# The bias table of a decoder trunk: 128 replicas copied from DRAM by GpSimd's queue instead of from one SBUF partition by ScalarE's

## The chip, the cores and the metric

The kernel runs on one core of one Trainium2 chip. The metric is device time in microseconds (us). Before the change three runs took 2225.4, 2230.37 and 2230.59 us, with a median of 2230.37 us. The engines of a core are named as in the profile: PE (TensorE, matrix products), PEld (its weight loads), DVE (VectorE), ACT (ScalarE), POOL (GpSimd) and SP (SyncE, which here only starts transfers). "ACTq" and "SPq" in a row are the queues of ACT and SP themselves: rows in which the engine's instruction stream is held by a transfer that it issues.

## The reference, cut to what matters

The reference is a trunk of two layers, 512 tokens of width 1024. Each layer has three sub-layers, each followed by a layer norm: a gated feed-forward block (FFN), a mixer of parallel head groups (sparse attention, spatial gating, a state-space scan), and a second FFN. Each sub-layer's input and output are scaled and shifted by vectors that come from a conditioning vector `c` through a large matrix `ada_w`.

```
mod = (silu(c) @ ada_w[l] + ada_b[l]).reshape(Bn, N_SUB, 3, D_MODEL)
h = x * (1.0 + scale[:, 0]) + shift[:, 0]
y = swiglu(h, ffn_w1[l, 0], ffn_w3[l, 0], ffn_w2[l, 0])
x = layer_norm(ALPHA * x + 0.5 * (1.0 + gate[:, 0]) * y, ...)
...
bias = rel_bias[rel_bucket(query position - key position)]   # 32 buckets, 8 heads
```

The bias of attention depends only on the distance between query and key and on the head. It is the same for both layers.

## The kernel before, in words

All matrix products are made of three products of split operands (`mm3`, lines 120 to 123): a high part and a low remainder of each side. The high part of a weight tile is made by ACT (`whi`, line 103), the low part by DVE (`wlo`, line 105), from a tile `raw` of 128 x 1024 that SP's queue has loaded. `raw` has four buffers.

An FFN (function `ffn`, 22 inner tiles in two halves of 11) does per inner tile f: two loads and splits (`w1`, `w3`), two projections of 24 matmuls each, then the gate: a tanh on ACT (line 292), two operations on DVE (lines 293 and 294, tile `th`), a high part on ACT (line 297, `ghi`) and a low part on DVE (line 298, `glo`). The weights of the next f are fetched and split while PE works on this one. After the 11 tiles of a half the products with `w2` follow (tile `y`), whose weights are first multiplied by a gain on DVE (line 101).

Beside that a background generator (`make_bg`) is advanced once per f. In the first FFN it has 71 parts over 19 calls: 63 belong to seven conditioning vectors (per vector eight loads of 512 KB of `ada_w`, each followed by a dot product on DVE at line 155, and a closing part), and eight belong to `make_bias`. `make_bias` stands behind the fifth vector, so that it runs in the second half of the first FFN. It multiplies the 33 x 8 bias table by a one-hot matrix of distances (line 390), copies the 8 x 640 result to the SBUF tile `row` (line 391), one head per partition, and then writes for each head 128 copies of its row of 640 numbers to the DRAM tensor `lane` (line 395), one transfer per part. The mixers later load from `lane` a 128 x 512 tile `T` per head in which each partition's row is shifted by one (line 88, called from `lane_load`); the replicas make that possible with one transfer. Everything that `make_bias` makes is needed in the mixer only.

A scheduler orders the instructions of each engine in advance; within an engine they then start in that order. The reciprocal roots of the layer norm run on POOL (line 219), which has nothing else to do before the first mixer.

Of the kernel before, what the change touches and what calls it, by code (L numbers as in the profile page):

```python
# [10 lines left out]
F32 = mybir.dt.float32  # L11
# [19 lines left out]
BLANE = 640  # L31
# [20 lines left out]
def kernel(ctx: ExitStack, tc: tile.TileContext, a: dict, out: bass.AP,  # L52
                             subs=((0, 0), (0, 1), (0, 2), (1, 0), (1, 1), (1, 2))):
    nc = tc.nc
    V, S, G, PE = nc.vector, nc.scalar, nc.gpsimd, nc.tensor
# [10 lines left out]
    dram = ctx.enter_context(tc.tile_pool(name="dram", bufs=1, space=DRAM))  # L66
# [10 lines left out]
    def big(s):  # L77
        return bp.tile([128, 1024], F32, tag="b", name=nm(s))

    def tiny(s, n, dt=F32):  # L80
        rot = s in ("mx", "sm", "fc", "st", "mv", "rs", "nr", "gst", "ss")
        return (t4 if rot else t1).tile([128, n], dt, tag=f"t_{s}", name=nm(s))

    def bank(k, s):
        return psp[k].tile([128, 512], F32, tag=k, name=nm(s))

    def load(dst, src):
        nc.sync.dma_start(dst, src)

    def bcast_row(src, n):  # L90
        return bass.AP(tensor=src.tensor, offset=src.offset, ap=[[0, 128], [1, n]])
# [6 lines left out]
    def wsplit(src, n=1024, gain=None):  # L98
        raw = raw_t(src, n)
        if gain is not None:  # L100
            V.tensor_mul(raw, raw, gain)  # L101
        hi = wp.tile([128, 1024], F32R, tag="hi", name=nm("whi"))
        S.copy(hi[:, :n], raw[:, :n])  # L103
        lo = wp.tile([128, 1024], F32R, tag="lo", name=nm("wlo"))
        V.tensor_sub(lo[:, :n], raw[:, :n], hi[:, :n].bitcast(F32))  # L105
        return hi, lo
# [15 lines left out]
        PE.matmul(o, lh, rl, start=False, stop=False)  # L122
        PE.matmul(o, ll, rh, start=False, stop=last)  # L123

    # constants
    cst = const.tile([128, 512], F32, name="cst")
    load(cst, a["cst"])
    ident = cst[:, 0:128]
# [18 lines left out]
        V.scalar_tensor_tensor(csil, c_th, 1.0, csil, op0=ALU.add, op1=ALU.mult)  # L147
        cond["c"] = csil

    # adaLN vectors, as columns  # L150
    mods = {}

    def ada_dot(acc, raw, l, v, k):
# [37 lines left out]
        V.tensor_mul(BB, sc, BB)  # L191
        V.tensor_add(BB, BB, sh)

    # modulated, transposed and split operand of the next projection
    def spread(b, z, P, banks):
        tiles = []
        for q in range(2):
            ps = bank(banks[q], "hps")
            for i in range(4):
                k = 4 * q + i  # L200
                PE.transpose(ps[:, i * 128:(i + 1) * 128], z[:, k * 128:(k + 1) * 128], ident)
            tiles.append(ps)
        for q in range(2):
            t = slab("hsum", "q")
            t3 = t.rearrange("p (k t) -> p k t", k=4)
            for i in range(4):
                sl = slice(i * 128, (i + 1) * 128)
                k = slice(4 * q + i, 4 * q + i + 1)
                if k.start in DVE_MOD:
                    V.tensor_scalar(t[:, sl], tiles[q][:, sl], P["GA"][:, k], P["BB"][:, k], op0=ALU.mult, op1=ALU.add)  # L210
                else:
                    S.activation(t[:, sl], tiles[q][:, sl], AF.Identity, bias=P["BB"][:, k], scale=P["GA"][:, k])
            hh = hT_hi[:, b, 4 * q:4 * q + 4, :]
            S.copy(hh, t3)
            V.tensor_sub(hT_lo[:, b, 4 * q:4 * q + 4, :], t3, hh.bitcast(F32))  # L215
# [161 lines left out]
        flush(P)  # L377
        renew(P)

    # T5 bias by distance, causal  # L380
    def make_bias():
        rb = tiny("rb", 8)
        load(rb[0:32, :], a["rel_bias"])
        V.memset(rb[32:33, :], NEG)
        oh = big("oh")
        load(oh[0:33, 0:BLANE], a["onehot"])
        row = big("row")
        for q, n in ((0, 512), (1, 128)):
            ps = bank("Y", "rowps")
            PE.matmul(ps[0:8, :n], rb[0:33, :], oh[0:33, q * 512:q * 512 + n], start=True, stop=True)  # L390
            V.tensor_copy(row[0:8, q * 512:q * 512 + n], ps[0:8, :n])
        d = dram.tile([8, 128, BLANE], F32, name="lane")
        for h in range(8):
            yield
            S.dma_start(d[h], row[h:h + 1, 0:BLANE].unsqueeze(1).to_broadcast([1, 128, BLANE]))
        lane.append(d)

    def gelu2(dst, src, n):
# [7 lines left out]
    def mixer(l, P, last, lane, params):  # L406
# [15 lines left out]
        G.affine_select(w3v, w3v, pattern=[[0, 4], [1, 128]], compare_op=ALU.is_ge, fill=0.0, base=0,  # L422
                        channel_multiplier=-1)

        # token-major columns
        wa = [wsplit(a["wA"][l, :, c * 852:c * 852 + n], n) for c, n in ((0, 852), (1, 852), (2, 568))]
        wb = [wsplit(a["wB"][l, :, c * 1024:(c + 1) * 1024]) for c in range(2)]
        dtx, gts = tiny("dtx", 16), tiny("gts", 96)
# [36 lines left out]
            project(ps, wsplit(a["wS"][l, i]))  # L465
            return ps

        # work for the tensor engine in small parts, put between those of the attention
        pre = {}

        def fetch(i):
# [11 lines left out]
                    yield  # L483
            return ps

        # state-space inputs
        def conv(i, y):
            ps = proj(i)
            V.tensor_scalar(y, ps, cw[:, i * 4 + 3:i * 4 + 4], cw[:, 24 + i:25 + i], op0=ALU.mult, op1=ALU.add)
            for j in range(1, 4):  # L490
                V.scalar_tensor_tensor(y[:, j:], ps[:, :T - j], cw[:, i * 4 + 3 - j:i * 4 + 4 - j], y[:, j:],
                                       op0=ALU.mult, op1=ALU.add)
            th = slab("cth", "q")
            S.activation(th, y, AF.Tanh)
            V.scalar_tensor_tensor(y, th, 1.0, y, op0=ALU.add, op1=ALU.mult)
# [21 lines left out]
        def pair(t):  # L517
            return [t[:, 0:512], t[:, 512:1024]]
# [15 lines left out]
            S.activation(y, ps, AF.Tanh, scale=0.5)  # L534
            V.scalar_tensor_tensor(y, y, 1.0, ps, op0=ALU.add, op1=ALU.mult)

        # spatial gating
        def spatial(i):
            if not og:
                og.extend(pair(big("og")))  # L540
            ps = yield from proj_parts(8 + i)
            u = og[i]
            S.copy(u, ps)
            gelu2(u, u, 512)
            sv = bank("Y", "sv")
            for b in range(4):
                for j in range(2):
                    g = 2 * i + j
                    PE.matmul(sv[j * 64:(j + 1) * 64, b * 128:(b + 1) * 128],
                              gv[b // 2][:, (b % 2) * 256 + g * 64:(b % 2) * 256 + (g + 1) * 64],  # L550
                              wsT[:, g * 128:(g + 1) * 128], start=True, stop=True)
            t = slab("svb", "q")
            V.tensor_add(tok(t, 0, 4), tok(sv, 0, 4),
                         bs[:, i * 128:(i + 1) * 128].unsqueeze(1).to_broadcast([128, 4, 128]))
            V.scalar_tensor_tensor(u, t, 0.5, u, op0=ALU.mult, op1=ALU.mult)

        # queries, stacked high over low (low over high for the second group); keys: high parts in both halves, low once
        Q, K = {}, {}
        lo_half, hi_half = slice(0, 64), slice(64, 128)

# [34 lines left out]
        between = [({"h": hidden, "q": query, "k": key}[c[0]], int(c[1])) for c in CORE_FILL.split()]  # L595
# [3 lines left out]
                f, i = between.pop(0)  # L599
                f(i)  # L600

        # step sizes and their sums
        dt, aa = tiny("dt", 16), tiny("aa", 16)
        u, r, z2, pl = tiny("du", 16), tiny("dr", 16), tiny("dz", 16), tiny("dp", 16)
        V.scalar_tensor_tensor(u, dtx, -1.0, dtx, op0=ALU.mult, op1=ALU.max)
# [6 lines left out]
        for d in (15, 13, 11, 9, 7, 5, 3):  # L612
# [15 lines left out]
                  start=False, stop=True)  # L628
        cs = tiny("cs", 16)
        V.tensor_copy(cs, cps[:, 0:16])  # L630

        # token-major inputs and states
        Xt = pair(big("Xt"))
        for i in range(2):
            ps = bank("H", "xtp")
# [13 lines left out]
        for c in range(2):  # L649
            for g in range(2):  # L650
                cb = bank("H", "cb")
                for j in range(2):
                    h = 2 * g + j
# [4 lines left out]
                    for n, part_ in enumerate(a2):  # L658
                        PE.matmul(o[:, 128:256], part_[:, k0 + 4:k0 + 5].to_broadcast([128, 128]), trio_r[:, 0:128],
                                  start=False, stop=(n == 1))  # L660
# [5 lines left out]
                          start=True, stop=True)  # L666
# [10 lines left out]
                for j in range(2):  # L677
                    h = 2 * g + j
# [75 lines left out]
        for q in range(2):  # L754
            PE.matmul(ps[:, 0:64], w2k[:, q * 128:(q + 1) * 128], gT[:, q * 128:q * 128 + 64],
                      start=(q == 0), stop=(q == 1))
# [235 lines left out]
        flush(P)  # L992
        renew(P)

    # start
    P0 = {"GA": tiny("GA", 8), "BB": tiny("BB", 8)}
    ab = [tiny(f"ab{j}", 8) for j in range(2)]
    acc = [tiny(f"acc{j}", 8) for j in range(2)]
# [79 lines left out]
    for n, (l, s) in enumerate(subs):  # L1078
        last = n == len(subs) - 1
        P = {}  # L1080

        def params():
            norm_par(l, s, P)
            if (l, s, 2) in mods:
                gate_par(l, s, P)
            if not last and (*subs[n + 1], 0) in mods:
                next_par(l, s, *subs[n + 1], P)

        if s == 1:
            if not lane:  # L1090
                for _ in make_bias():
                    pass
            need(l, s, 2)
            if not last:
                need(*subs[n + 1], 1)
                need(*subs[n + 1], 0)
            cond.clear()
            mixer(l, P, last, lane, params)
        else:
            if share.get(n) and "c" not in cond:  # L1100
                silu_c()
            after_mixer = n > 0 and subs[n - 1][1] == 1
            ffn(l, s, P, last, make_bg(n, P), (2, 0) if after_mixer and QORDER[0] == 3 else (0, 2), params,
                feed if n == 0 else None)
# [87 lines left out]
```

## Time and profile before

| | before |
|---|---|
| runs, us | 2225.4, 2230.37, 2230.59 |
| median, us | 2230.37 |
| span of the profiled execution, us | 2225.3 |
| PE busy | 2099.0 us, 94% |
| DVE busy | 1345.0 us, 60% |
| ACT busy | 776.2 us, 35% |
| POOL busy | 24.1 us, 1% |
| mean granted TensorE clock | 0.978 |

The page gives the span as the profiled execution's time; it is 0.1 us under the fastest run and 5.1 us under the median. PE is busy nearly all the time, so what can be gained lies where PE is not busy. The page's second part shows the busy tenths in 40 slices of 55.6 us. PE has 9 almost everywhere, apart from the first slice (6), the third (7), the last (7) and the sixth to eighth (4, 5, 7), which are the stretch from 278 to 445 us. The granted clock of these three reads 7, 7, 8 where it is 9 elsewhere. This stretch is where `make_bias` runs.

### The profile page before, as it was taken

What the parts mean: (1) busy time and instruction counts of PE and PEld (TensorE: products, weight loads), DVE (VectorE), ACT (ScalarE), POOL (GpSimd) and SP (SyncE); (2) the same over time, 40 slices, a digit from 0 to 9 for tenths busy, and PEclk for the clock granted to TensorE, in tenths of its full rate; (3) what the DMA queues carried; (4) which work ended last, traced back from release to release, by engine and by line L of the source; (5) the groups of instructions that cost most, each with busy time, mean ns of one, the idle gap of its engine ahead of it and who ended that gap; (6) DMA issues with size and microseconds to landing.
All of it is one profiled execution on the core that took longest, in us unless ns stands there. A gap on an engine that the chain in (4) does not pass through costs nothing.

```text
span 2225.3 us, 26047 instructions
## 1 busy us (share of the span) xinstructions
PE 2099.0 (94%) x10024; PEld 1667.4 (75%) x10024; DVE 1345.0 (60%) x2416; ACT 776.2 (35%) x1351; POOL 24.1 (1%) x34
## 2 busy tenths in 40 slices
PE   6979945799999999999999999999999999999997
PEld 5868834588766688888888878888876668888886
DVE  6784612768676686544766645566867676453363
ACT  4221201343455652222334222224345565222232
POOL 0000000000000000000000000000000000000000
PEclk9999977899999999999999999999999999999999
DMA  8763778622421146345445635532241113223331
GB/s 326 222 224 104 228 77 77 198 95 86 152 67 48 39 160 206 108 143 151 136 139 186 184 104 170 168 114 90 90 147 67 48 39 114 95 95 96 102 96 38
DMA packets 93480, 279.71 MB, mean 126 GB/s; under 512 B 19211, under 2 KB 23563, under 8 KB 93356
## 3 DMA queue, kind: packets, MB, share of 16 engines
q1 hardware_dynamic: 92204, 275.43, 38.1%
q10 hardware_dynamic: 1152, 2.62, 3.5%
q8 instruction: 79, 1.29, 0.2%
q14 instruction: 45, 0.37, 0.1%
HBM read 273.27 MB, written 4.74 MB: 125 GB/s over the span
## 4 chain that ended last, share of the span: by engine, by line
PE 74%; DMA 12%; DVE 8%; issue 3%; ACT 2%; ACTq 1%; POOL 0%; SPq 0%; DVEq 0%; POOLq 0%
PE h L122 9%; PE h L121 9%; PE h L123 9%; PE y L121 8%; PE y L123 8%; PE y L122 7%; DMA raw<-in_ada_w_dram 7%; DMA raw<-in_w_dram 3%; PE pj L121 3%; PE pj L122 3%; PE pj L123 3%; PE op L900 3%; PE tp L890 2%; PE S L860 2%; DVE raw L155 2%
## 5 line engine op out<-in xcount | busy, mean ns | idle before, releaser
L121 PE MATMUL h<-hT_hi,whi 128*128 128x512 f32 (+1 forms) x1488 | 561.6, 379 | 60.5 <-ACT whi L103 55.8
L103 ACT CAST whi<-raw 128x1024 fp32r<-128x1024 f32 (+1 forms) x306 | 317.9, 1046 | 719.8 <-issue 197.7
L123 PE MATMUL h<-hT_hi,wlo 128*128 128x512 f32 (+1 forms) x1488 | 561.6, 377 | 0.4 <-DVE wlo L105 0.4
L122 PE MATMUL h<-hT_lo,whi 128*128 128x512 f32 (+1 forms) x1488 | 561.7, 377 | 0.3 <-DVE hT_lo L215 0.3
L105 DVE TENSOR_TENSOR wlo<-raw,whi 128x1024 fp32r<-128x1024 f32 (+1 forms) x306 | 370.5, 1215 | 222.8 <-ACT whi L103 222.0
L121 PEld LDWEIGHTS h<-hT_hi,whi 128*128 128x128 f32 x1488 | 281.4, 189 | 113.5 <-ACT whi L103 57.3
L123 PEld LDWEIGHTS h<-hT_hi,wlo 128*128 128x128 f32 x1488 | 281.7, 189 | 53.7 <-DVE wlo L105 2.5
L122 PEld LDWEIGHTS h<-hT_lo,whi 128*128 128x128 f32 x1488 | 281.9, 189 | 51.4 <-DVE hT_lo L215 0.7
L155 DVE CUSTOM_DVE_ANT_0 raw<-raw,csil 128x1024 f32<-128x1024 f32 x144 | 174.8, 1221 | 199.9 <-DMA raw<-in_ada_w_dram 199.1
L121 PE MATMUL y<-whi,ghi 128*128 128x512 f32 x576 | 228.2, 396 | 30.5 <-DVE th L294 26.1
L122 PE MATMUL y<-wlo,ghi 128*128 128x512 f32 x576 | 227.1, 394 | 1.8 <-DVE wlo L105 1.8
L123 PE MATMUL y<-whi,glo 128*128 128x512 f32 x576 | 226.6, 393 | 0.0
L101 DVE TENSOR_TENSOR raw<-raw,G 128x1024 f32<-128x1024 f32 x86 | 104.6, 1222 | 85.2 <-DMA raw<-in_w_dram 85.0
L121 PEld LDWEIGHTS y<-whi,ghi 128*128 128x128 f32 x576 | 109.9, 191 | 57.8 <-DVE th L294 30.3
L297 ACT CAST ghi<-th 128x512 fp32r<-128x512 f32 x88 | 54.5, 620 | 240.7 <-DVE th L294 230.4
L122 PEld LDWEIGHTS y<-wlo,ghi 128*128 128x128 f32 x576 | 109.8, 191 | 25.3 <-DVE wlo L105 2.8
L123 PEld LDWEIGHTS y<-whi,glo 128*128 128x128 f32 x576 | 109.7, 190 | 23.1
L121 PE MATMUL pj<-hT_hi,whi 128*128 128x512 f32 x288 | 118.5, 411 | 0.0
L123 PE MATMUL pj<-hT_hi,wlo 128*128 128x512 f32 x288 | 113.5, 394 | 0.0
L122 PE MATMUL pj<-hT_lo,whi 128*128 128x512 f32 x288 | 113.1, 393 | 0.0
L294 DVE TENSOR_TENSOR th<-th,h 128x512 f32<-128x512 f32 x88 | 60.0, 683 | 41.4 <-PE h L123 40.3
L892 ACT COPY pt<-tp 128x512 f32<-128x512 f32 (+2 forms) x96 | 54.6, 581 | 85.3 <-PE tp L890 76.5
(288 smaller groups left out, 2564.0 us busy)
## 6 DMA issues: line engine op xcount, KB each, us to landing
raw<-in_w_dram SPq DMA_DIRECT2D x264, 512.0 KB, 3.7
raw<-in_ada_w_dram SPq DMA_DIRECT2D x144, 512.0 KB, 4.5
raw<-in_wS_dram SPq DMA_DIRECT2D x36, 512.0 KB, 4.2
raw<-in_cw_dram SPq DMA_DIRECT2D x16, 512.0 KB, 4.1
raw<-in_wo_dram SPq DMA_DIRECT2D x16, 512.0 KB, 3.5
T<-lane SPq DMA_DIRECT2D x16, 256.0 KB, 4.0
lg<-in_ln_g_dram SPq DMA_DIRECT2D x6, 512.0 KB, 6.9
lb<-in_ln_b_dram SPq DMA_DIRECT2D x6, 512.0 KB, 6.8
```

The lines of the kernel that those rows point to most:

```text
L101: V.tensor_mul(raw, raw, gain)
L103: S.copy(hi[:, :n], raw[:, :n])
L105: V.tensor_sub(lo[:, :n], raw[:, :n], hi[:, :n].bitcast(F32))
L121: PE.matmul(o, lh, rh, start=first, stop=False)
L122: PE.matmul(o, lh, rl, start=False, stop=False)
L123: PE.matmul(o, ll, rh, start=False, stop=last)
L155: V.tensor_tensor_reduce(out=raw, in0=raw, in1=cond["c"], scale=0.5, scalar=0.0, op0=ALU.mult, op1=ALU.add, accum_out=acc[:, k:k + 1])
L294: V.tensor_mul(th, th, h3)
L297: S.copy(hi, th)
L860: PE.matmul(o, Q[g, i][r, qs], K[br][1][r, :nk], start=False, stop=True)
L892: S.copy(pt[0:n, :], tp[0:n, :])
L900: PE.matmul(op[r, :], v, pt[0:n, g * 256:(g + 1) * 256], start=(br == 0), stop=(br == 2 and kb == qb))
```

## The change

The 8 x 640 result in SBUF is copied once to a DRAM tensor `table` (20 KB, one transfer), and the eight transfers that write the 128 replicas per head read their row from there, by an access pattern that names the same 640 numbers 128 times. All nine are issued by GpSimd's queue; ACT issues none. (The rest of the diff removes comments and leaves blank lines.)

```diff
             PE.matmul(ps[0:8, :n], rb[0:33, :], oh[0:33, q * 512:q * 512 + n], start=True, stop=True)
             V.tensor_copy(row[0:8, q * 512:q * 512 + n], ps[0:8, :n])
+        t = dram.tile([8, BLANE], F32, name="table")
+        G.dma_start(t[:, :], row[0:8, 0:BLANE])
         d = dram.tile([8, 128, BLANE], F32, name="lane")
         for h in range(8):
             yield
-            S.dma_start(d[h], row[h:h + 1, 0:BLANE].unsqueeze(1).to_broadcast([1, 128, BLANE]))
+            G.dma_start(d[h], bcast_row(t[h], BLANE))
         lane.append(d)
```

The lines behind it move by two: line 395 becomes 397, and the transfer of the table is line 393.

On ACT, in the second half of the first FFN, before the change (`whi` is the high part of a weight tile, `th` and `ghi` belong to the gate):

```order
L103 CAST whi_2059<-raw_2057 128x1024
L297 CAST ghi_1913<-th_1909 128x512
L395 DMA lane<-row_1923 128x1x640 x2
L292 ACTIVATE th_1995<-h_337_1933 128x512
L395 DMA lane<-row_1923 128x1x640
L297 CAST ghi_1999<-th_1995 128x512
L395 DMA lane<-row_1923 128x1x640 x3
L103 CAST whi_2065<-raw_2063 128x1024
L292 ACTIVATE th_2069<-h_348_2007 128x512
L395 DMA lane<-row_1923 128x1x640
L297 CAST ghi_2073<-th_2069 128x512
L395 DMA lane<-row_1923 128x1x640
```

Six of the eight transfers stand ahead of the cast of the second weight tile of the next f (`whi_2065`). The same place on ACT after the change:

```order
L103 CAST whi_2061<-raw_2059 128x1024
L297 CAST ghi_1913<-th_1909 128x512
L103 CAST whi_2067<-raw_2065 128x1024
L292 ACTIVATE th_1997<-h_337_1935 128x512
L103 CAST whi_2145<-raw_2143 128x1024
L297 CAST ghi_2001<-th_1997 128x512
L103 CAST whi_2151<-raw_2149 128x1024
L292 ACTIVATE th_2071<-h_348_2009 128x512
```

The eight transfers are gone from ACT, and the casts of the next weight tiles stand between the steps of the gate (the tile that was `whi_2065` is `whi_2067` here).

On DVE, from the copy of the bias row on, before the change (`ISA` at line 155 is the dot product of a loaded tile of `ada_w`):

```order
L391 COPY row_1923<-rowps_1927 8x128
L155 ISA raw_2088,mod_360_2079<-raw_2088,csil_112 128x1024
L155 ISA mod_360_2079 128x1
L155 ISA raw_2161,mod_360_2079<-raw_2161,csil_112 128x1024
L155 ISA mod_360_2079 128x1
L155 ISA raw_2164,mod_360_2079<-raw_2164,csil_112 128x1024
L155 ISA mod_360_2079 128x1
L155 ISA raw_2167,mod_360_2079<-raw_2167,csil_112 128x1024
L155 ISA mod_360_2079 128x1
L293 SCALAR_TENSOR_TENSOR th_1995<-th_1995,h_337_1933 128x512
L294 TENSOR_TENSOR th_1995<-th_1995,h_338_1934 128x512
```

The gate's two operations stand behind four dot products in a row. The same place on DVE after the change:

```order
L391 COPY row_1923<-rowps_1927 8x128
L155 ISA raw_2090,mod_360_2081<-raw_2090,csil_112 128x1024
L155 ISA mod_360_2081 128x1
L105 TENSOR_TENSOR wlo_2069<-raw_2065,whi_2067 128x1024
L293 SCALAR_TENSOR_TENSOR th_1997<-th_1997,h_337_1935 128x512
L155 ISA raw_2163,mod_360_2081<-raw_2163,csil_112 128x1024
L155 ISA mod_360_2081 128x1
L155 ISA raw_2166,mod_360_2081<-raw_2166,csil_112 128x1024
L155 ISA mod_360_2081 128x1
L294 TENSOR_TENSOR th_1997<-th_1997,h_338_1936 128x512
```

Now the first of the two stands behind one dot product and the second behind three, and the low part of the next weight tile has moved ahead of them.

On POOL, before its first reciprocal root (`mv`, line 219, which becomes the same line after), after the change:

```order
L393 DMA table<-row_1923 8x640
L397 DMA lane<-table 128x640 x8
L219 ISA
L219 TENSOR_TENSOR mv_2701<-mv_2701,mhalf 128x1
```

Before the change POOL had no transfer here; now its first reciprocal root stands behind nine of them. The eight copies of the heads follow each other with no other instruction between them.

## Rows read from the trace of the kernel before

**Rows 1.** Busy time of each engine in five stretches, from the windows view: start and end, length, PE, PEld, DVE, ACT and POOL busy us (with the count of instructions), granted TensorE clock as a share, mean DMA share, GB/s.

```profile
140.00:180.00 40.00, 26.94 (x110) 21.27 (x109) 26.06 (x27) 10.04 (x11) 0.00 (x0) 0.87 0.39 129
180.00:280.00 100.00, 100.00 (x440) 81.84 (x439) 55.05 (x76) 24.10 (x28) 0.00 (x0) 1.00 0.57 177
300.00:400.00 100.00, 43.74 (x161) 33.38 (x160) 28.10 (x41) 11.57 (x15) 0.00 (x0) 0.71 0.84 98
310.00:340.00 30.00, 1.00 (x2) 0.50 (x2) 5.46 (x8) 2.16 (x3) 0.00 (x0) 0.50 0.69 72
400.00:440.00 40.00, 27.26 (x102) 21.05 (x101) 30.63 (x35) 11.73 (x15) 0.00 (x0) 0.79 0.58 177
```

**Rows 2.** PE in order of time, from the timeline: the last matmul before the two long gaps and the first one behind each (start, duration, and in brackets the idle time before it with what ended it).

```profile
301.99 0.39 PE L123 MATMUL h<-hT_hi,wlo 128*128 128x512 f32 x1
339.00 0.80 PE L121 MATMUL h<-hT_hi,whi 128*128 128x512 f32 x1 [36.63 <-ACT whi L103]
...
346.79 0.39 PE L123 MATMUL h<-hT_hi,wlo 128*128 128x512 f32 x1
362.26 0.79 PE L121 MATMUL h<-hT_hi,whi 128*128 128x512 f32 x1 [15.08 <-ACT whi L103]
```

**Rows 3.** ACT and its queue in order of time from 273 us on.

```profile
273.64 1.05 ACT L103 CAST whi<-raw 128x1024 fp32r<-128x1024 f32 x1 [3.89 <-issue]
278.27 0.62 ACT L297 CAST ghi<-th 128x512 fp32r<-128x512 f32 x1 [3.58 <-DVE th L294]
280.79 9.52 ACTq L395 DMA_DIRECT2D lane<-row  x2
290.41 0.60 ACT L292 ACTIVATE th<-h 128x512 f32<-128x512 f32 x1 [11.53 <-issue]
290.44 1.05 ACTq L395 DMA_DIRECT2D lane<-row  x1
327.85 0.62 ACT L297 CAST ghi<-th 128x512 fp32r<-128x512 f32 x1 [36.84 <-DVE th L294]
327.86 10.01 ACTq L395 DMA_DIRECT2D lane<-row  x3
337.91 1.04 ACT L103 CAST whi<-raw 128x1024 fp32r<-128x1024 f32 x1 [9.44 <-issue]
338.02 11.58 ACTq L395 DMA_DIRECT2D lane<-row  x1
338.86 0.59 ACT L292 ACTIVATE th<-h 128x512 f32<-128x512 f32 x1
349.64 0.62 ACT L297 CAST ghi<-th 128x512 fp32r<-128x512 f32 x1 [10.19 <-issue]
349.66 11.46 ACTq L395 DMA_DIRECT2D lane<-row  x1
361.16 1.99 ACT L103 CAST whi<-raw 128x1024 fp32r<-128x1024 f32 x2 [10.91 <-issue]
```

**Rows 4.** DVE in order of time from 280 to 390 us, the rows whose wait was ended by a transfer.

```profile
307.76 1.22 DVE L155 CUSTOM_DVE_ANT_0 raw<-raw,csil 128x1024 f32<-128x1024 f32 x1 [25.87 <-DMA raw<-in_ada_w_dram]
320.07 1.23 DVE L155 CUSTOM_DVE_ANT_0 raw<-raw,csil 128x1024 f32<-128x1024 f32 x1 [11.07 <-DMA raw<-in_ada_w_dram]
325.19 1.23 DVE L155 CUSTOM_DVE_ANT_0 raw<-raw,csil 128x1024 f32<-128x1024 f32 x1 [3.89 <-DMA raw<-in_ada_w_dram]
386.06 1.23 DVE L155 CUSTOM_DVE_ANT_0 raw<-raw,csil 128x1024 f32<-128x1024 f32 x1 [15.97 <-DMA raw<-in_ada_w_dram]
```

**Rows 5.** The transfers from 281 to 387 us: q10 is ACT's queue, q1 is SP's (packets, MB, share of the time of 16 DMA engines in this stretch), then issues with their count, KB each and median us to landing.

```profile
q10 hardware_dynamic: 1152, 2.62, 73.4%
q1 hardware_dynamic: 1248, 4.55, 11.6%
...
raw<-in_ada_w_dram SPq DMA_DIRECT2D x6, 512.0 KB, 22.5
lane<-row ACTq DMA_DIRECT2D x8, 320.0 KB, 26.4
```

**Rows 6.** The transfers from 220 to 260 us, in the same form.

```profile
q1 hardware_dynamic: 3674, 9.09, 79.2%
...
raw<-in_ada_w_dram SPq DMA_DIRECT2D x10, 512.0 KB, 4.6
```

**Rows 7.** The transfers from 36 to 50 us, among them two (`lg`, `lb`) in which 128 partitions read the same row of 4 KB from DRAM.

```profile
DMA packets 1999, 5.11 MB, mean 365 GB/s; under 512 B 307, under 2 KB 819, under 8 KB 1998
...
q1 hardware_dynamic: 1998, 5.10, 94.5%
...
raw<-in_w_dram SPq DMA_DIRECT2D x2, 512.0 KB, 10.5
lg<-in_ln_g_dram SPq DMA_DIRECT2D x1, 512.0 KB, 10.5
lb<-in_ln_b_dram SPq DMA_DIRECT2D x1, 512.0 KB, 10.4
```

**Rows 8.** The transfers from 2195 to 2225 us, which write the result from 128 partitions to DRAM.

```profile
q1 hardware_dynamic: 1152, 2.10, 18.7%
...
out_dram<-x_sb SPq DMA_DIRECT2D x8, 256.0 KB, 2.0
```

**Rows 9.** The chain of waits that ended last, from 270 to 400 us, its shares by line.

```profile
by line: DMA raw<-in_ada_w_dram 58.0%; ACTq L395 15.6%; issue 9.5%; DVE raw L155 5.7%; DMA raw<-in_w_dram 3.3%; DVE wlo L105 2.8%; ACT whi L103 2.4%; DVE th L294 2.1%; DVE th L293 0.9%; ACT ghi L297 0.9%; DVE row L391 0.6%; DVE glo L298 0.5
```

**Rows 10.** POOL's first reciprocal root, from the timeline of POOL.

```profile
467.29 0.55 POOL L219 TENSOR_TENSOR mv<-mv,mhalf 128x1 f32<-128x1 f32 x1 [466.78 <-DVE mv L218]
```

**Rows 11.** The first loads that read the replicas, from the timeline of SP's queue.

```profile
481.64 1.81 SPq L88 DMA_DIRECT2D T<-lane  x4
```

## The prediction

> **What bounds the kernel now.** I read the busy tenths of the page first: PE is busy nearly everywhere but in one stretch in the first quarter, and the granted clock falls there too. So the second view is the windows around that stretch [rows 1]. From 180 to 280 us PE is 100% busy at clock 1.00 and does 440 matmuls; from 300 to 400 us it does 161 at a mean of 0.71, and from 310 to 340 us two, at 0.50, which is the 1.2 GHz level of the 1.2 and 2.4 GHz. The reader is to see that this is lost PE time in the middle of an FFN that otherwise keeps PE full, not a stage with another limit. The two transitions from projections to the `w2` products (140 to 180 and 400 to 440 us) lose less, and about the same: 110 and 102 matmuls in 40 us.
>
> Third, the timeline of PE: it runs dry at 302 us, and both long gaps (36.63 and 15.08 us) are ended by the same thing, the cast of a weight tile on ACT [rows 2]. Fourth, the timeline of ACT says why the cast is late [rows 3]. ACT's own work is small, but the eight transfers of line 395 hold its stream for 9.52 + 1.05 + 10.01 + 11.58 + 11.46 = 43.6 us, 5.5 us each, and the `ghi` cast at 327.85 waits 36.84 us for DVE. So fifth, DVE: its dot products wait 25.87, 11.07, 3.89 and 15.97 us for loads of `ada_w` [rows 4], and the gate stands behind them in order. Sixth, the transfers: from 281 to 387 us the 16 engines spend 73.4% of their time on ACT's queue for only 2.62 MB, while the loads of `ada_w` take 22.5 us to land [rows 5], against 4.6 us in an undisturbed stretch [rows 6]. Two things therefore hold PE up, one behind the other: ACT's stream is held by issuing, and the loads that DVE needs crawl because the DMA engines are full of replicas. The chain of waits of this stretch has them both: 58.0% loads of `ada_w`, 15.6% ACT's queue and 9.5% "issue" [rows 9].
>
> How slow the replicas are: 2.62 MB in 106 us is 24.7 GB/s, and a packet holds an engine for 0.734 x 106 x 16 / 1152 = 1.08 us. SP's packets in the same stretch take 0.116 x 106 x 16 / 1248 = 0.16 us [rows 5]. All replicas of one head read the same SBUF partition.
>
> **The change part by part.**
>
> *The eight issues leave ACT.* 43.6 us of held stream go from ACT [rows 3], and the casts stand between the steps of the gate as everywhere else. Their worth isn't 43.6 us: it is what PE lost, and it must be counted together with the next part.
>
> *The replicas come from DRAM.* What is removed is the read side, one partition; the write side (the same 2.62 MB to DRAM) stays. The trace has no copy from DRAM to DRAM, so I bound it. From below: reads in which 128 partitions take one row of DRAM run at full rate; in a stretch with two of them among four loads the mean is 365 GB/s, and a packet takes 0.945 x 14 x 16 / 1998 = 0.106 us [rows 7]. 1152 packets on 16 engines are then 7.6 us of all engines. From above, for a copy that is as good on both sides as the nearest rows: writes to DRAM take 0.187 x 30 x 16 / 1152 = 0.078 us a packet [rows 8]; a read and a write one behind the other are 0.184 us, or 13.2 us. The far end is that nothing gets better, 1.08 us a packet and 77.8 us; that is the first rival. I take 7.6 to 13.2 us, since rows for each side speak for it and none shows a slow write to DRAM.
>
> The Trainium skill (SBUF — State Buffer, Door 1: The DMA port swizzle) says that DMA rate goes by how many of 16 ports the partitions reach, and gives 27.6 GB/s measured for partitions 0 to 3, which share one port. The 24.7 GB/s here agree with it. By that rule the read side is the whole cost and a DRAM source is free of it; by a limit on the write side the first rival would come true.
>
> *Does this burst stall PE?* POOL has no other work there, so the eight copies are issued at once and not over 70 us. Normally q1 takes 79.2% of the engines with PE full [rows 1, 6]. While the generator gives its eight parts to the replicas, about two f, it starts no dot products, so up to eight loads of 512 KB are late in coming, some 8 x 0.52 / 365 GB/s = 11 us of the engines. 7.6 to 13.2 us of new work against 11 us that moves away: nearly even. What does come late meets a cover: PE went on for 302 - 280.8 = 21 us after ACT had stopped [rows 2, 3]. So the residue is between 0 and 13 us, and I take 3 us, near the end with the cover. If the cover is gone, it costs the whole 13.
>
> *The table's transfer* (20 KB) is waited for by POOL's queue alone. Behind it stand the eight copies, and behind these the reciprocal roots, the first at 467 us [rows 10]; the replicas are read from 481.64 us on [rows 11]. Both come some 60 us earlier afterwards, about 404 and 418. Nobody waits: 0. From below I see no gain either, since POOL idles.
>
> *PE's time.* A window of 100 us at 440 matmuls does 4.40 per us. The 161 matmuls from 300 to 400 us are worth 161 / 4.40 = 36.6 us, so 63.4 us are lost there [rows 1]; the slow clock is already in this count. What is late next is the transition: it lost 40 - 102 / 4.40 = 16.8 us with the disturbance ahead of it and 40 - 110 / 4.40 = 15.0 us in the first half without it. It stays, within 2 us.
>
> Sum, against the profiled execution: 2225.3 - 63.4 + 3 = 2164.9 us. Its span is 5.1 us under the median of the runs, two of which stand at 2230; against the median I forecast 2230.4 - 60.4 = 2170 us.
>
> **The rivals.**
>
> *First: the DMA engines stay clogged.* The Trainium skill (DMA: Bandwidth & Descriptors, Issuing engines are not separate DMA queues) says that transfers issued by ACT, SP or GpSimd run on the same 16 engines and that another issuer saves issue time only. If writing 128 rows to DRAM is what costs 1.08 us a packet, or if 128 reads of one row collide, the loads of `ada_w` crawl on and only ACT is free. Then the gain is at most what the chain puts on ACT: 15.6% + 9.5% of 130 us = 33 us [rows 9], down to nothing where DVE's waits cover it: 2197 to 2230, say 2212 us. For it: q10 fills the engines. Against it: broadcast reads at 365 GB/s and writes at 0.078 us a packet [rows 7, 8]. An in-between case, a burst that stalls PE by 13 to 30 us, gives 2180 to 2197.
>
> *Second: the time moves nowhere.* The lost 63 us could be due to the loads of `ada_w` alone, too many for this half. Then nothing changes: 2230. Against it: 180 to 280 us has the same generator and PE is full [rows 1].
>
> *Third: slower, by POOL's order.* The first reciprocal root, on which the layer norm and so PE wait, stands behind nine transfers on POOL. The room is 404 - 281 = 123 us (the issues began at 280.79), or 13.7 us per transfer; from there the norm is late, and from (123 + 63) / 9 = 20.7 us per transfer on the kernel is slower than before. At 25 us each it would be 225 - 123 - 63 = 39 us slower, 2269. For it: ACT's issues took up to 11.58 us [rows 3]. Against it: they took so long on a clogged queue, and the mean was 5.5. The Trainium skill (SBUF — State Buffer, the "DVE blocks DMA" trap) says that descriptors of GpSimd's queue are written by its own cores and wait while DVE holds a shared port. No run here shows that; DVE is busy for 55% of an undisturbed stretch [rows 1], which leaves room for them.
>
> **How the numbers follow.** The forecast, with its residue of 0 to 13 us, has 0.80; the clogged case 0.08 and the in-between case 0.06; no change 0.03; POOL's order 0.03. A change under 0.3% (7 us) can't be told from none here. Faster by more than that: forecast, in-between case and most of the clogged case, 0.92. Same: 0.05. Slower: 0.03. The range: its low end is the fastest run less the whole loss and half of the second transition, 2225.4 - 63.4 - 8 = 2154. Its high end takes in the in-between case: 2197.
>
> **What would show it.** In the profile afterwards PE should be near 100% busy at clock 1.00 from 280 to about 335 us, with the transition at about 340; no row of ACT's queue; GpSimd's copies with under 0.2 us a packet, landed by about 310 us; loads of `ada_w` landing in 5 to 10 us there. A gap of PE ended by a DVE wait for `ada_w` while GpSimd's queue fills the engines would show the clogged case. A wait for line 219 near 404 us would show POOL's order. I am wrong if the time is over 2197 us.

## The result and the profile after

The changed kernel took 2163.26 us (median of four runs, 2162.17 to 2167.9), the kernel before 2230.32 us beside it: a ratio of 0.970, with an interval from 0.9685 to 0.9718. The forecast was 2170 us, between 2154 and 2197. The profiled execution has a span of 2161.5 us and a mean granted clock of 0.989.

The windows view of the changed kernel, with the columns of [rows 1]:

```profile
280.00:300.00 20.00, 20.00 (x90) 16.53 (x90) 11.62 (x18) 5.18 (x7) 4.90 (x9) 1.00 0.90 312
300.00:340.00 40.00, 40.00 (x178) 33.14 (x177) 27.80 (x40) 10.11 (x13) 0.00 (x0) 1.00 0.69 205
300.00:400.00 100.00, 87.53 (x370) 71.34 (x369) 58.22 (x73) 24.77 (x33) 0.00 (x0) 0.91 0.52 160
340.00:380.00 40.00, 27.52 (x106) 21.63 (x105) 23.23 (x25) 10.32 (x14) 0.00 (x0) 0.79 0.38 124
```

The hole is gone. From 300 to 400 us PE does 370 matmuls where it did 161 [rows 1], and until 340 us it is busy without a break at clock 1.00. What is left is the transition to the `w2` products, now at 340 to 380 us: 106 matmuls in 40 us, so 40 - 106 / 4.40 = 15.9 us lost.

The transfers of the changed kernel from 281 to 320 us, in the form of [rows 5]; q0 is GpSimd's queue:

```profile
q1 hardware_dynamic: 2352, 8.08, 60.9%
q0 software_dynamic: 672, 2.64, 19.3%
...
raw<-in_ada_w_dram SPq DMA_DIRECT2D x12, 512.0 KB, 4.6
lane<-table POOLq DMA_DIRECT2D x8, 320.0 KB, 6.9
raw<-in_w_dram SPq DMA_DIRECT2D x4, 512.0 KB, 7.3
```

The replicas are the same 2.62 MB, but they take 0.193 x 39 = 7.5 us of all 16 engines and not 0.734 x 106 = 77.8 us [rows 5]. Beside them the loads of `ada_w` land in 4.6 us, as in an undisturbed stretch [rows 6], not in 22.5. The loads of weights (`in_w`) take 7.3 us. A replica's packet costs 0.193 x 39 x 16 / 672 = 0.18 us; the packets are larger than those of ACT's queue were (672 for 2.64 MB, before 1152 for 2.62).

POOL in order of time:

```profile
281.29 0.72 POOL L393 DMA_DIRECT2D table<-row  x1 [280.77 <-DVE row L391]
285.30 4.18 POOL L397 DMA_DIRECT2D lane<-table  x8 [3.29 <-DMA table<-row]
402.02 0.56 POOL L219 TENSOR_TENSOR mv<-mv,mhalf 128x1 f32<-128x1 f32 x1 [112.55 <-DVE mv L218]
```

POOL waits 3.29 us for the table, starts eight copies in 4.18 us (0.52 us each), and then idles for 112.55 us until its first reciprocal root. That root waits for DVE, not for transfers. It comes 467.29 - 402.02 = 65.3 us earlier than in [rows 10], and the whole span is 63.8 us shorter: all of the gain lies ahead of it. Behind the root both kernels take nearly the same time, 2161.5 - 402.0 = 1759.5 and 2225.3 - 467.3 = 1758.0 us.

ACT and DVE, from the timelines of the changed kernel, for [rows 3] and [rows 4]:

```profile
285.50 1.05 ACT L103 CAST whi<-raw 128x1024 fp32r<-128x1024 f32 x1 [3.89 <-PE h L122]
290.94 1.05 ACT L103 CAST whi<-raw 128x1024 fp32r<-128x1024 f32 x1 [0.32 <-PE h L122]
...
299.59 1.05 ACT L103 CAST whi<-raw 128x1024 fp32r<-128x1024 f32 x1 [7.11 <-DMA raw<-in_w_dram]
...
296.51 1.23 DVE L155 CUSTOM_DVE_ANT_0 raw<-raw,csil 128x1024 f32<-128x1024 f32 x1 [4.81 <-DMA raw<-in_ada_w_dram]
```

Until 299 us the casts of the weight tiles wait for PE to free a tile, so ACT is ahead of PE; before, PE waited for these casts [rows 2]. The cast at 299.59 waits 7.11 us for its load, which matters below. DVE's longest wait for `ada_w` from 280 to 340 us is 4.81 us, not 25.87.

### The profile page after: what moved, and what is told of

Its sections match the earlier page's. It is cut to its first block, busy times and chain, and to the rows that moved or that the text cites. A ratio compares the mean times of both kernels' runs of the same rounds, so it can differ in the third digit from the quotient of the medians.

```text
span 2161.5 us, 26067 instructions
## 1 busy us (share of the span) xinstructions
PE 2092.3 (97%) x10024; PEld 1664.9 (77%) x10024; DVE 1344.4 (62%) x2416; ACT 775.9 (36%) x1351; POOL 29.0 (1%) x43
## 3 DMA queue, kind: packets, MB, share of 16 engines
q0 software_dynamic: 672, 2.64, 0.3%
## 4 chain that ended last, share of the span: by engine, by line
PE 77%; DMA 10%; DVE 8%; issue 3%; ACT 2%; POOL 0%; SPq 0%; DVEq 0%; POOLq 0%; ACTq 0%
PE h L122 10%; PE h L121 10%; PE h L123 10%; PE y L121 8%; PE y L123 8%; PE y L122 8%; DMA raw<-in_ada_w_dram 5%; DMA raw<-in_w_dram 4%; PE pj L121 3%; PE pj L122 3%; PE pj L123 3%; PE op L902 3%; PE tp L892 2%; DVE wlo L105 2%; PE S L862 2%
## 5 line engine op out<-in xcount | busy, mean ns | idle before, releaser
L894 ACT COPY pt<-tp 128x512 f32<-128x512 f32 (+2 forms) x96 | 54.6, 581 | 85.4 <-PE tp L892 76.9
```

Source lines behind the costliest of these rows:

```text
L894: S.copy(pt[0:n, :], tp[0:n, :])
```

## The experiments

The theory: the single source partition is the cause. The read side slows the copies, the slow copies fill the 16 DMA engines, and both holds of PE (ACT's stream, which cannot issue on, and the late loads of `ada_w`) follow from that. The rival: the issuer is the cause, and a copy from anywhere would hold ACT and so PE. A second question was what the remaining burst costs, since the prediction gave it 3 us without a row that shows it. In the edits `G` is GpSimd and `S` is ACT; `...` stands for lines left out. Apart from the first, whose edit is against the kernel before, and one that names its own base, the edits are against the changed kernel.

### The issuer alone, and the source alone

First the issuer: GpSimd copies from the one SBUF partition, with no table.

```diff
-            S.dma_start(d[h], row[h:h + 1, 0:BLANE].unsqueeze(1).to_broadcast([1, 128, BLANE]))
+            G.dma_start(d[h], row[h:h + 1, 0:BLANE].unsqueeze(1).to_broadcast([1, 128, BLANE]))
```

> One part alone: GpSimd's queue issues the eight copies, but they still read one SBUF partition each, with no table in DRAM. Theory (the slow thing is reading one partition, and it clogs the 16 engines for every queue): a packet of the copies still takes about 1 us, 2.6 MB go at about 25 GB/s, loads of ada_w land in over 15 us beside them, PE still has a gap of 10 us or more ended by a DVE or ACT wait that goes back to a load; 2190 to 2225 us. Rival (ACT's held stream was the cost): as the changed kernel, 2160 to 2168 us, with PE full from 280 to 340 us.

It took 2247.08 us against 2231.34 for before in that set: 1.0073 of it [1.0056, 1.0089]. It is slower, which neither side had said: my forecast of 2190 to 2225 us is missed. Its transfers from 281 to 375 us:

```profile
q0 software_dynamic: 640, 2.62, 79.3%
q1 hardware_dynamic: 1005, 3.64, 10.3%
...
raw<-in_ada_w_dram SPq DMA_DIRECT2D x5, 512.0 KB, 16.5
lane<-row POOLq DMA_DIRECT2D x8, 320.0 KB, 54.6
```

Its DVE and PE in order of time (rows whose wait is long):

```profile
310.44 1.23 DVE L155 CUSTOM_DVE_ANT_0 raw<-raw,csil 128x1024 f32<-128x1024 f32 x1 [26.34 <-DMA raw<-in_ada_w_dram]
346.94 1.22 DVE L155 CUSTOM_DVE_ANT_0 raw<-raw,csil 128x1024 f32<-128x1024 f32 x1 [35.26 <-DMA raw<-in_ada_w_dram]
370.44 1.23 DVE L155 CUSTOM_DVE_ANT_0 raw<-raw,csil 128x1024 f32<-128x1024 f32 x1 [19.94 <-DMA raw<-in_ada_w_dram]
```

```profile
348.91 0.76 PE L121 MATMUL h<-hT_hi,whi 128*128 128x512 f32 x1 [46.79 <-DVE th L294]
380.01 0.77 PE L121 MATMUL h<-hT_hi,whi 128*128 128x512 f32 x1 [17.41 <-DVE th L294]
```

ACT issues nothing here, and PE is dry for 46.79 and 17.41 us all the same, now ended by the gate on DVE. The copies take 0.793 x 94 = 74.5 us of all engines, as before. Taking the issues from ACT even hurts. POOL queues all eight within 4.31 us, while ACT's held stream had spread them over 70 us [rows 3], and DVE waits up to 35.26 us for one load; that the crowding makes these waits longer is the likely reason, not tried by itself. The first root comes at 474.87 us, 7.6 later than in [rows 10]. The rest of its loss lies behind the root (2246.8 - 474.9 = 1771.9 us, 14 more than in before).

That second loss is one of order. Its timeline shows the transposes of the first normed block late, behind products that could have waited:

```profile
494.81 1.97 PE L201 MATMUL hps<-cst,z 128*128 128x128 f32 x8 [5.61 <-ACT z L255]
```

So I ran the same kernel with the products of the last group in the later blocks held until those transposes are issued (the edit beside the change of the issuer):

```diff
+    turned = []
...
-                PE.transpose(ps[:, i * 128:(i + 1) * 128], z[:, k * 128:(k + 1) * 128], ident)
+                turned.append(PE.transpose(ps[:, i * 128:(i + 1) * 128], z[:, k * 128:(k + 1) * 128], ident).ins)
...
-                    for f, w in zip(fs[-RES:], ws):
-                        down(f, w, b, (q,))
+                    behind = feed and half and b >= 2 and q == 1
+                    with tc.issue_after(turned[-1]) if behind else ExitStack():
+                        for f, w in zip(fs[-RES:], ws):
+                            down(f, w, b, (q,))
```

> The run in which only the issuer was changed (copies by GpSimd from one SBUF partition) came out slower than before, and part of that was lost at 490 to 510 us, where its order on PE put the transposes of the first normed block behind all products of the FFN. Here the same copies by GpSimd, with the transposes of a block put ahead of the last products of the FFN's later blocks, as in the other kernels. Theory (two separate losses: the clog as before, and the order): the 14 us behind the first reciprocal root go, the clog stays; 2228 to 2238 us, no faster than before. Rival (the clog itself did it all): 2243 us or more.

It took 2238.2 us, 1.0044 of before [1.0022, 1.0067], 0.2 us over the upper end of the forecast. In the profiled execution the stretch behind the root falls to 2232.6 - 473.2 = 1759.4 us, as elsewhere, so there the 14 us were the order. But the six runs spread from 2232.99 to 2247.86 us and the profiled one (2234.34) is the second fastest; two of the others, at 2244.89 and 2247.86, are as slow as without the new order, and what they lost is not known. PE's long waits stay:

```profile
355.68 0.76 PE L121 MATMUL h<-hT_hi,whi 128*128 128x512 f32 x1 [55.09 <-DVE th L296]
378.19 0.76 PE L121 MATMUL h<-hT_hi,whi 128*128 128x512 f32 x1 [9.20 <-DVE th L296]
```

Then the source alone: ACT's queue moves the table and copies from it.

```diff
-        G.dma_start(t[:, :], row[0:8, 0:BLANE])
+        S.dma_start(t[:, :], row[0:8, 0:BLANE])
...
-            G.dma_start(d[h], bcast_row(t[h], BLANE))
+            S.dma_start(d[h], bcast_row(t[h], BLANE))
```

> The other part alone: the table goes to DRAM and the copies read it there, but ACT issues all nine transfers. Theory (source is the cause): the copies are as fast as in the changed kernel, the issues hold ACT for about 0.5 us each and some 4 us for the table to land, under 10 us in all, which is less than the 21 us that PE can go on; 2161 to 2170 us. Rival (issuing on ACT holds it 5.5 us each whatever the source): 40 us or more of held stream, PE gaps of 15 us or more, 2180 to 2210 us.

It took 2162.62 us, 0.969 of before [0.9674, 0.9708]: the whole gain. Its windows, then its ACT queue in order of time:

```profile
280.00:300.00 20.00, 20.00 (x90) 16.56 (x89) 11.81 (x20) 5.40 (x7) 0.00 (x0) 1.00 0.87 274
300.00:340.00 40.00, 40.00 (x178) 33.16 (x177) 27.39 (x40) 9.46 (x12) 0.00 (x0) 1.00 0.77 228
...
283.59 0.56 ACTq L393 DMA_DIRECT2D table<-row  x1
286.48 1.21 ACTq L397 DMA_DIRECT2D lane<-table  x2
287.81 7.55 ACTq L397 DMA_DIRECT2D lane<-table  x5
296.75 0.48 ACTq L397 DMA_DIRECT2D lane<-table  x1
```

The nine issues hold ACT for 9.8 us, against the 43.6 us of [rows 3], and PE is full at clock 1.00 from 280 to 340 us here as well. The hold of ACT was an effect of the slow source. The theory stands, and the issuer by itself is worth nothing here.

### What of the source is slow

GpSimd's queue again, without the table in DRAM: the product puts the same row of a head on 128 partitions, and each copy reads every partition once.

```diff
-        row = big("row")
-        for q, n in ((0, 512), (1, 128)):
-            ps = bank("Y", "rowps")
-            PE.matmul(ps[0:8, :n], rb[0:33, :], oh[0:33, q * 512:q * 512 + n], start=True, stop=True)
-            V.tensor_copy(row[0:8, q * 512:q * 512 + n], ps[0:8, :n])
-        t = dram.tile([8, BLANE], F32, name="table")
-        G.dma_start(t[:, :], row[0:8, 0:BLANE])
         d = dram.tile([8, 128, BLANE], F32, name="lane")
         for h in range(8):
             yield
-            G.dma_start(d[h], bcast_row(t[h], BLANE))
+            row = big("row")
+            for q, n in ((0, 512), (1, 128)):
+                ps = bank("Y", "rowps")
+                PE.matmul(ps[:, :n], rb[0:33, h:h + 1].to_broadcast([33, 128]), oh[0:33, q * 512:q * 512 + n],
+                          start=True, stop=True)
+                V.tensor_copy(row[:, q * 512:q * 512 + n], ps[:, :n])
+            G.dma_start(d[h], row[:, 0:BLANE])
         lane.append(d)
```

> GpSimd's queue copies from SBUF again, but from 128 partitions: per head the product with the one-hot matrix is made with the head's column repeated 128 times, so that each partition holds the row and each replica is read from its own partition. PE does 8 products instead of 1, at 1.24 us each some 9 us more, and DVE 16 copies instead of 2. Theory (one partition is slow, SBUF is not): copies at 0.1 to 0.3 us a packet, no gap of PE; the changed kernel plus 5 to 12 us, 2166 to 2176 us. Rival (any SBUF source is slow beside the loads, only DRAM to DRAM is free): about 1 us a packet and 2190 us or more.

It took 2170.02 us, 0.973 of before [0.9714, 0.9743], as forecast. From 270 to 400 us:

```profile
q0 software_dynamic: 640, 2.62, 5.0%
```

0.050 x 130 x 16 / 640 = 0.16 us a packet: an SBUF source is not slow if it is spread. Three further kernels, each run once beside one run of before of 2229.81 us, read fewer partitions: 0 to 3, 0 to 15, and every eighth one (0, 8, ..., 120). The edit of the third, against the kernel that reads 128:

```diff
-            G.dma_start(d[h], row[:, 0:BLANE])
+            G.dma_start(d[h].rearrange("(a b) n -> a b n", a=16),
+                        row[0:128:8, 0:BLANE].unsqueeze(1).to_broadcast([16, 8, BLANE]))
```

> As the run that reads 128 partitions (product per head, GpSimd issues from SBUF), but each head's copies read only partitions 0 to 3, 32 replicas from each. Four neighbouring partitions share one port by the Trainium skill (SBUF — State Buffer, Door 1: The DMA port swizzle). By a limit per port the copies go no faster than from one partition, about 25 GB/s or 0.2 us per KB and engine of four: packets of 5 KB at 0.7 to 0.8 us on four engines; by a limit per partition (25 GB/s each) they are four times as fast, packets at 0.2 us. No forecast of the total better than 2170 to 2260 us.

> The same with partitions 0 to 15, eight replicas from each, on 16 engines. By a limit per port (these are four ports by the same section): about 100 GB/s, 0.7 to 0.8 us per packet of 5 KB, some 25 us for all copies; by a limit per partition: 0.2 us per packet, as from 128 partitions. Total 2170 to 2200 us.

> The same with 16 partitions that are eight apart (0, 8, 16, ... 120), which are eight ports by the same section. By a limit per port: about 200 GB/s, 0.35 to 0.4 us per packet of 5 KB, half of the run with partitions 0 to 15; by a limit per partition: no difference between the two. Total 2168 to 2185 us.

They took 2231.42, 2175.66 and 2162.95 us; the third is 5 us under its forecast. The issues of the first from 270 to 400 us, where each copy runs nearly by itself:

```profile
lane<-row POOLq DMA_DIRECT2D x6, 320.0 KB, 15.8
```

328 KB in 15.8 us are 20.7 GB/s from four partitions, no more than from one (24.7 in before). Four times the partitions bought no rate. This run differs in two more ways, which were not tried apart: its copies kept only about four engines busy (15.8% of 16 engines over 130 us are 329 us of engine time, for about five copies of 15.8 us), and their packets were of about 1 KB. The second and the third, from 270 to 400 us, have packets of 4 KB and their edits differ in nothing but the partitions:

```profile
q0 software_dynamic: 640, 2.62, 14.2%
```

```profile
q0 software_dynamic: 640, 2.62, 6.2%
```

That is 0.46 us a packet from 16 neighbours and 0.20 us from 16 partitions that lie apart. So it counts which partitions are read, and not only how many; whether it is their distance or a fixed grouping, these runs do not show. The Trainium skill (SBUF — State Buffer, Door 1: The DMA port swizzle) says that DMA rate goes by the ports that the partitions reach; the order of the three agrees with it. By the engines' time both sixteens were faster than I had worked out beforehand, 2.62 MB in 0.142 x 130 = 18.5 us and in 0.062 x 130 = 8.1 us, or 142 and 325 GB/s against about 100 and 200.

The third needs no trip through DRAM and in its one run is level with the changed kernel, though its rows of products cost PE time from 260 to 340 us. Its transition, 340 to 380 us, loses almost nothing:

```profile
340.00:380.00 40.00, 38.66 (x171) 31.70 (x170) 25.51 (x28) 11.42 (x15) 0.00 (x0) 1.00 0.40 116
```

Why that is was not tried, nor why the kernel that reads 128 partitions, with the cheaper packets, took 7 us more.

### What the burst costs

Only head 0's copy is made, and all heads read it; seven copies are left out.

```diff
-        d = dram.tile([8, 128, BLANE], F32, name="lane")
+        d = dram.tile([1, 128, BLANE], F32, name="lane")
         for h in range(8):
             yield
-            G.dma_start(d[h], bcast_row(t[h], BLANE))
-        lane.append(d)
+            if h == 0:
+                G.dma_start(d[0], bcast_row(t[0], BLANE))
+        lane.append([d[0]] * 8)
```

> The changed kernel with one of its eight copies: only head 0 gets its 128 replicas, and all heads read those (the other seven copies are left out, so the bias of the other heads is not theirs). Theory (the burst of copies costs nothing, since PE is covered): the same as the changed kernel within 0.3%, 2157 to 2169 us, and no more than 2 us under it. Rival (the burst still delays loads by the 3 to 13 us that the prediction allowed): 3 us or more faster, under 2160 us.

It took 2158.76 us (2158.14 to 2164.86), 4.5 us under the changed kernel's 2163.26; the profiled spans differ by 2161.5 - 2156.6 = 4.9 us. My forecast for a free burst is missed. The medians alone do not show that the burst costs something: the two kernels ran in different sets, and their runs overlap (2158.14 to 2164.86 against 2162.17 to 2167.9 us). The traces do. Where it is paid is seen from 340 to 380 us:

```profile
340.00:380.00 40.00, 31.25 (x129) 25.43 (x128) 22.41 (x25) 11.21 (x16) 0.00 (x0) 0.87 0.39 117
```

129 matmuls, a loss of 40 - 129 / 4.40 = 10.7 us where the changed kernel loses 15.9. From 280 to 340 us both are full. The long waits of PE in this stretch, two in the changed kernel and then one with a single copy:

```profile
344.44 0.79 PE L121 MATMUL y<-whi,ghi 128*128 128x512 f32 x1 [3.04 <-DVE th L294]
355.52 0.80 PE L121 MATMUL y<-whi,ghi 128*128 128x512 f32 x1 [9.43 <-DVE th L294]
```

```profile
351.86 0.80 PE L121 MATMUL y<-whi,ghi 128*128 128x512 f32 x1 [8.75 <-DVE th L294]
```

The loads that the burst delays reach PE here, some 40 us later. The loads of weights before the change from 220 to 260 us, where nothing disturbs them, and with one copy from 281 to 320 us:

```profile
raw<-in_w_dram SPq DMA_DIRECT2D x8, 512.0 KB, 4.4
```

```profile
raw<-in_w_dram SPq DMA_DIRECT2D x5, 512.0 KB, 4.4
```

In the changed kernel they took 7.3 us there; DVE waited 4.81 us for `ada_w` at 296.51 us and ACT 7.11 us for a weight tile at 299.59. With one copy no wait for either load is over 2.9 us from 280 to 330 us. So the gate falls behind: its `ghi` casts follow each other by 15.7 us (289.99 to 305.66), and by 11.4 with one copy (291.73 to 303.13). PE has work until the transition, where it needs the gate of the last tile. The first reciprocal root gives the price without the noise of what follows: it comes at 397.6 us with one copy, and at 402.0, 403.6 and 404.9 us in the three profiled executions with the whole burst from DRAM at about 285 us (the changed kernel twice, and ACT as its issuer).

The other direction, each copy made six times (the further five into DRAM that nobody reads), and for the same set of runs the changed kernel again:

```diff
+        more = [dram.tile([8, 128, BLANE], F32, name=f"more{i}") for i in range(5)]
         for h in range(8):
             yield
-            G.dma_start(d[h], bcast_row(t[h], BLANE))
+            for e in [d] + more:
+                G.dma_start(e[h], bcast_row(t[h], BLANE))
```

> The changed kernel with each of the eight copies made six times (five more copies per head to DRAM tensors that nobody reads): 15.7 MB instead of 2.6, at 7.4 us of all 16 engines per set some 44 us of engine time, issued at once by GpSimd. Theory (the burst is paid in engine time that the loads of ada_w and of the weights then lack, less the 11 us of loads that stay away, some 12 us of spare time of the engines, and what PE has in hand): 5 to 25 us slower than the changed kernel, 2168 to 2190 us, with DVE waiting for ada_w. Rival (GpSimd's transfers from DRAM don't hold up SP's loads): 2160 to 2167 us.

> The changed kernel itself, on the same chip as the other runs of this set, as the measure for them: 2160 to 2168 us.

They took 2217.75 us (0.9945 of before [0.993, 0.996]) and 2162.08 us (0.9693 [0.9678, 0.9707]). Five further sets cost 55.7 us, 11.1 each; I had expected 5 to 25 in all. The transfers with six copies from 281 to 387 us:

```profile
q0 software_dynamic: 3832, 15.61, 57.1%
q1 hardware_dynamic: 3907, 11.66, 36.5%
...
raw<-in_ada_w_dram SPq DMA_DIRECT2D x13, 512.0 KB, 11.5
```

A set takes 0.571 x 106 / 6 = 10.1 us of all engines and costs 11.1 us of time once the engines are full (57.1% and 36.5% of them here). The first set costs less than half of that, which fits with engine time that was still free (about 20% in the changed kernel from 281 to 320 us).

Last, the burst moved: SP's queue issues the copies behind the last loads of weights of the FFN's second half.

```diff
+    late, loads = [], []
+
     def raw_t(src, n=1024):
         raw = wp.tile([128, 1024], F32, tag="raw", name=nm("raw"), bufs=4)
-        load(raw[:, :n], src)
+        loads.append(nc.sync.dma_start(raw[:, :n], src).ins)
...
+            if half and late:
+                t, d = late.pop()
+                with tc.issue_after(loads[-1]):
+                    for h in range(8):
+                        load(d[h], bcast_row(t[h], BLANE))
...
         for h in range(8):
             yield
-            G.dma_start(d[h], bcast_row(t[h], BLANE))
+        late.append((t, d))
```

> The changed kernel with the eight copies moved: the table is still written by GpSimd at 281 us, but the copies are issued by SP behind the last weight loads of the FFN's second half, at about 360 us, where the 16 engines are busy for 0.41 of the time. Theory (the burst costs the 4 to 5 us by which the kernel with one copy was faster, paid in the transition at 340 us): as that kernel, 2156 to 2161 us. Rival (the one-copy kernel was faster by chance or by its shorter total): as the changed kernel, 2162 to 2168 us.

It took 2157.86 us (2156.91 to 2159.57), 0.968 of before [0.9662, 0.9691]: 4.2 us under the changed kernel of the same set, and the lowest median of all. The intervals of the two ratios overlap a little, so the medians alone would not settle it. The windows do point the same way (this kernel first, the changed kernel again second):

```profile
340.00:380.00 40.00, 32.12 (x133) 26.10 (x132) 20.84 (x24) 11.07 (x16) 0.00 (x0) 0.87 0.54 169
```

```profile
340.00:380.00 40.00, 26.23 (x103) 20.69 (x102) 22.07 (x23) 9.24 (x13) 0.00 (x0) 0.79 0.42 123
```

Losses of 9.8 and 16.6 us, and the first root comes at 395.8 us against 403.6; the later copies meet an FFN whose loads have been issued.

## Why the prediction was right

*What bounds the kernel.* Right. Both holds of PE came from the slow copies, and the two kernels that change the issuer alone and the source alone show that the copies' read side was behind both.

*The issues leave ACT.* Right in that their worth was not to be counted by itself: taken away alone they gave nothing, and the kernel became 0.7% slower, part of it by another order on PE.

*The replicas come from DRAM.* Bounded at 7.6 to 13.2 us of all engines, measured 7.5, just under the lower end. The bound took 1152 packets at 0.106 to 0.184 us; GpSimd's queue made 672 larger ones at 0.18. On ACT's queue the same copies were 1168 packets with the table's, 20.6% of the engines from 281 to 320 us, so 0.206 x 39 x 16 / 1168 = 0.11 us each and 8.0 us in all; the total is near the lower bound with packets of either size. The rows of broadcast reads and of writes [rows 7, 8] had bounded an operation that the trace of before did not have. With the engines crowded, as with six sets, it is 10.1.

*PE's time.* 63.4 us were counted as lost from 300 to 400 us, to go entirely. PE is full until 340 us, and the span fell by 63.8.

*The transition and the residue.* Here two terms were wrong and offset each other, which was luck. The prediction let the transition stay at 15 to 17 us and added 3 us for the burst. Measured, the transition loses 9.8 to 10.7 us with no burst ahead of it, and the burst adds 5 to 7 there. Their sum, 15.9, is that of the transition alone in the prediction, so the 3 us of the sum were counted on top of it, about what the span came out under the forecast, 2164.9 - 2161.5 = 3.4 us. The prediction set what comes late against PE's cover of 21 us, in the stretch of the burst, and there PE indeed lost nothing; the delay was handed on to the next place without a cover. The transition of the first half loses 15 us with no copies at all [rows 1]; why the second could do better is open.

*POOL's wait.* Right: first root at 402.0 us (404 forecast) and the replicas read from 416.4 us (418). No engine but POOL waits for the nine transfers, and POOL (3.29 us, for the table) has time.

*The sum against the median.* Of the 6.7 us by which 2170 was too high, 3.4 are the term above. The other 3.3 are the base: the profiled execution of before was 5.1 us under its median, that of the changed kernel is 1.8 us under its own.

*The rivals.* The clogged engines did not come, because the slowness was on the read side; with the source unchanged that rival comes true, and more than it foresaw, as it had no case in which freeing ACT makes the queueing worse. "Nowhere" is out: the loads of `ada_w` were not too many, they were crowded out. POOL's order is out: 0.52 us an issue, where 20.7 were needed for a loss; with the slow source too, eight issues held POOL for only 4.31 us.

## What to carry to other kernels

When a queue holds an engine at its issues, look at what the queue's transfers cost the DMA engines before moving them to another queue: if their source is slow, another issuer only queues them faster and the loads beside them wait longer. Broadcast from a DRAM row, or from partitions spread over all 128 (every eighth one here), rather than from one SBUF partition. A burst of transfers that costs nothing where it is issued can still be paid at the next transition, so place it behind the last loads that someone waits for; here that was worth about 4 us.

## What the runs showed of the hardware

A slow source on one queue slowed the loads of the other. The copies moved only 24.7 GB/s, but their packets sat on the 16 engines for 73% of the time, and loads from DRAM to other partitions took 22.5 us and not 4.6. The same transfer used 1152 packets from ACT's queue and 640 from GpSimd's, at 1.08 and 1.86 us each (0.793 x 94 x 16 / 640), so neither queue moves the row faster.

GpSimd's issues took 0.52 us each beside a DVE that was busy for 11.62 of 20 us, with no sign of one holding up the other. How long issuing holds an engine differed between the queues: beside the slow source eight issues held ACT for 43.6 us, and POOL for 4.31 us, though its copies took 54.6 us to land.
